# Moving background steps between the stages of the first section of a hybrid attention and retention trunk

## The chip, the cores and the metric

The kernel runs on one core of a Trainium2 chip. The metric is the device time of one execution, in microseconds (us). All times of the profile are of one execution on that core.

## The reference

The program is a trunk of two layers over a sequence of 2048 positions with 1024 features. Each layer normalises its input by its root mean square, projects it to eight groups of 512 columns, and feeds two mixers: chunked softmax attention (8 heads of 64 columns, each chunk of 64 positions seeing itself and the 8 chunks before it, with a relative bias) and multi-scale retention (4 heads of 128 columns, rotary phases, exponential decay from chunk to chunk). Both are gated, laid side by side, projected back and added to the input. Cut to what matters:

```python
hn = rms_norm(x, norm_gain)
proj = hn @ w_in                       # (2048, 1024) @ (1024, 4096)
aq, ak, av, ag, rq, rk, rv, rg = split(proj)
a = chunked_rel_attention(aq, ak, av, rel_bias) * silu(ag)
b = chunkwise_retention(rq, rk, rv, cos, sin) * silu(rg)
x = x + concat([a, b]) @ w_out         # and after two layers a last rms_norm
```

The rotary tables cos and sin are computed from the positions.

## The kernel before

All large products are made from 16-bit pieces: each operand is split in a high and a low part, and three products (high by high, high by low, low by high) are summed in PSUM.

A layer is done in four sections (s); a section is two attention heads and one retention head, 128 columns of each of the eight groups. Within a section the positions are done in four blocks (n) of 512. For each (layer, section, block) there are two stages on TensorE:

- the **T stage**, `dense_T` (L748): four products of 24 matmuls each, giving q, k, rq and rk with the columns on the partitions (tiles `dT`);
- the **V stage**, `dense_V` (L767): four products of 24 matmuls, giving v, rv and the gates with the positions on the partitions (tiles `dV`).

Each product is cut in three, so a stage has twelve "thirds" of 8 matmuls. After each third, `run()` does three things: it runs what had been put off to this third (`later`), it advances the attention generator of the block before by one step, and it pulls background steps. The attention generator brings the scores (matmuls L815 and L816; DVE L819 and L821; the exponential and a copy on ACT, L822 and L824; a subtraction on POOL, L825; a transposing DMA issued by SP, L827), the product with v (L835 to L837) and the retention (matmuls L869; copies on ACT L873; sums on DVE L877). A score unit has a name such as 2_1: the third run of 128 positions of the block, second head. Evacuations of the dense products are ACT and DVE instructions (L664, L667 and L681 in the T stage; L775 to L778 and L781 to L785 in the V stage). The rotary turn is three POOL instructions (L689 to L691).

The background steps are generators in a list, `bg`, and their order is the order in which they were pushed. At a third, `run()` pulls `ceil(todo / left)` steps, where `todo` is what remains of the pushed numbers of steps and `left` starts at the third argument of `run()` (the thirds over which the steps are to be spread) and falls by one with each third:

```python
            if bg:
                pull(min(-(-todo // max(left, 1)), todo))
            left -= 1
```

So a stage of twelve thirds that is run with 24 gets about half of what is outstanding, and one that is run with 12 gets all of it. A step issues its instructions at that point of the program, and each engine works through its instructions in program order. The order on each engine is thus set by these numbers.

In the first section of the first layer these are the background steps:

- `tables(n, ..)` (L85 to L128), for the rotary tables of a block: DVE steps, two sines on ACT (L117, L118; a load of the activation table stands before them and another when ACT goes back to its other functions), a negation (L120) and eight DMAs to memory (L125 to L128);
- `norms_from_input` (L1168 on), the input norms of four row tiles of 128 positions: load (L1177), a sum of squares on ACT (`sq`, L204), the mean on DVE (L209) and the power on POOL (L211), the multiplication on DVE (`mul`, L1189), the high part on ACT (`hi`, L226), the low part on DVE (`lo`, L230), and two transposing DMAs (L235, L236) into `hTh` and `hTl`, which the dense stages of that block read. At n = 1 they are for block 2 (row tiles 8 to 11), at n = 2 for block 3 (row tiles 12 to 15). In some of these steps the buffers of the high and low part are tiles named `rows`, in others tiles named `xa`;
- `prep_T` (25 steps), the weights of the next section for `dense_T`, in four parts: load (L297), a square with its sum on ACT (L312, its output goes to the tile `whT`), a cast on DVE (L319, `mbT`), a matmul with ones that adds over the partitions (L326, `msT`), a scale from it (L328, L143 to L147), and the two parts of the weights (L333 on ACT, `whT`; L336 on DVE, `wlT`);
- `prep_V` (23 steps), the same for `dense_V` (`msV` and so on), pushed at the last V stage of a section.

In the kernel before, `prep_T` of section 1 is pushed ahead of the T stage of block 3. T stages of this section are run with 10 (block 0), 22 (blocks 1 and 2) and 14 (block 3), V stages with 12, but with 24 for block 3.

Of the kernel before, what the change touches and what calls it, by code (L numbers as in the profile page):

```python
# [27 lines left out]
def hybrid_trunk(ctx: ExitStack, tc: tile.TileContext, x, pos, gain, gcol, w_in, w_out, rel, fgain,  # L28
# [6 lines left out]
    NS = SEQ // 512  # L35
    NSW = 4
# [348 lines left out]
    def prep_T(l, s, g, halves=False, w=None):  # L385
        w = w or Sections(l, s, g, halves)
        w.load(0)
        yield
        for j in range(4):
            if j < 3:  # L390
                w.load(j + 1)
            yield
            w.square(j)
            yield
            yield
            yield
            w.scale(j)
            yield from w.split(j)
# [208 lines left out]
    def later(k, fn):  # L607
        deferred.append([k, fn])
# [11 lines left out]
    def in_order(apart, terms):  # L620

        return [(kt, w) for w in terms for kt in range(KT)] if apart else [(kt, w) for kt in range(KT) for w in terms]
# [132 lines left out]
    def dense_V(l, s, n, g, st):  # L755
        hh, hl = hT[l, n]
        nm = f"{l}_{s}_{n}"
        st.v = b3.tile([P, 4, 2, 129], F16, tag="v", name=f"v{nm}")
        pool.memset(st.v[:, :, :, 64:65], 1.0)
        st.rv, st.g = [], []  # L760
        while g.vdone < 4:
            pull(1)
        for a in range(4):
            ps = psD.tile([P, 512], F32, tag="dense", name=f"dV{nm}_{a}")
            m = 0
            for kt, (w_, h_) in in_order(a == 0, ((g.vh, hh), (g.vh, hl), (g.vl, hh))):
                pe.matmul(ps, h_[:, kt, a * P:(a + 1) * P], w_[:, kt, :], start=(m == 0), stop=(m == 23))  # L767
                m += 1
                if m in (8, 16):
                    yield  # L770
            rv = gp.tile([P, 3, P], F16, tag="rv", name=f"rv{nm}_{a}")
            gt = gp.tile([P, 256], F32, tag="gt", name=f"gt{nm}_{a}")
            pv_ = ps[:, 0:P].rearrange("p (h d) -> p h d", h=2)
            vh_ = st.v[:, a, :, 0:64]
            act.activation(vh_, pv_, AF.Copy, scale=2.0 ** -16)  # L775
            act.activation(gt, ps[:, 256:512], AF.Tanh, scale=g.ugh[:, 0:1])
            act.activation(rv[:, 0], ps[:, P:256], AF.Copy, scale=g.urv[:, 0:1])
            act.activation(rv[:, 2], rv[:, 0], AF.Copy, scale=2.0 ** -11)  # L778

            def rests(a=a, ps=ps, pv_=pv_, vh_=vh_, rv=rv, gt=gt):  # L780
                dve.scalar_tensor_tensor(out=st.v[:, a, :, 65:129], in0=pv_, scalar=2.0 ** -16, in1=vh_,  # L781
                                         op0=ALU.mult, op1=ALU.subtract)
                dve.scalar_tensor_tensor(out=rv[:, 1], in0=ps[:, P:256], scalar=g.urv[:, 0:1], in1=rv[:, 0],
                                         op0=ALU.mult, op1=ALU.subtract)
                dve.scalar_tensor_tensor(out=gt, in0=gt, scalar=1.0, in1=ps[:, 256:512], op0=ALU.add, op1=ALU.mult)  # L785

            later(1, rests)
            st.rv.append(rv)
            st.g.append(gt)
            yield  # L790
# [342 lines left out]
    def push(gen, steps):  # L1133
        bg.append([gen, steps])

    def pull(k):
        for _ in range(k):
            while bg:
                try:
                    next(bg[0][0])  # L1140
                    bg[0][1] -= 1
                    break
                except StopIteration:
                    bg.pop(0)
# [7 lines left out]
    def grp(l, s):  # L1152
        if (l, s) not in groups:
            groups[l, s] = Grp()
        return groups[l, s]

    def run(gen, att, thirds):
        left = thirds
        for _ in gen:
            tick()  # L1160
            if att[0] is not None and next(att[0], att) is att:
                att[0] = None
            ring["att_done"] = att[0] is None
            todo = sum(max(b[1], 0) for b in bg)
            if todo == 0 and bg:
                todo = 1
# [3 lines that stand above are left out]
# [205 lines left out]
    att = [None]  # L1375
    for l in range(DEPTH):
        gO = [Grp(), Grp()]
        go = Grp()
        for s in range(NSW):
            g = grp(l, s)  # L1380
            for n in range(NS):
                first = (l, s, n) == (0, 0, 0)
                if not first:
                    st = St()
                    states[l, s, n] = st
                    dT = dense_T(l, s, n, g, st)
                else:
                    st = st0
                if n == 0 and not first:
                    bs, bt = bias_scratch(l, s), bias_tiles(l, s, g)  # L1390
                    later(1, lambda bs=bs: next(bs))
                    for k in (6, 10, 17, 21):
                        later(k, lambda bt=bt: next(bt))
                if (l, s) == (0, 0) and 0 < n < NS - 1:
                    if n == 1:
                        push(t1, TAB_STEPS - 7)
                    pairs = [xs0[0], w4.tile([P, D], F32, tag="w4", name="rows8") if n == 1 else xs0[1]]
                    pairs = [(w_[:, 0:D], w_[:, D:2 * D]) for w_ in (r_.bitcast(F16) for r_ in pairs)]
                    push(norms_from_input(range(4 * n + 4, 4 * n + 8), late[0:4] if n == 1 else None, pairs,
                                          tables(n + 1, [xs0[n + 1][:, i * 256:(i + 1) * 256] for i in range(4)])), 21)  # L1400
                if (l, s, n) == (0, 1, 1):
                    for l_ in range(1, DEPTH):
                        gr = gain_scale(l_)
                        later(2, lambda gr=gr: next(gr))
                        later(10, lambda gr=gr: next(gr))
                        later(18, lambda gr=gr: next(gr))
                if n == (NS - 1 if (l, s) == (0, 0) else 1):
                    if s + 1 < NSW:
                        push(prep_T(l, s + 1, grp(l, s + 1)), 25)
                    else:  # L1410
                        push(prep_O(l, 0, gO[0], go), 9)
                if n == NS - 1 and s == 1 and l + 1 < DEPTH:
                    gain_load(l + 1)
                if not first:
                    run(dT, att, 10 if n == 0 else 14 if (l, s, n) == (0, 0, NS - 1) else 22 if (l, s) == (0, 0) else 24)
                if n == NS - 1 and s == NSW - 1:
                    us = []
                    push(wout_first(l, go, us), 10)
                if n == 2 and s == 2:
                    push(prep_Omax(l, go), 13)  # L1420
                if n == NS - 1:
                    if s + 1 < NSW:
                        push(prep_V(l, s + 1, grp(l, s + 1)), 23)
                    else:
                        push(prep_O(l, 1, gO[1], go), 9)
                run(dense_V(l, s, n, g, st), att, 24 if n == NS - 1 and s < NSW - 1 else 12)
                if first:
                    sp_order.__exit__(None, None, None)
                    ring["free"] = True
                if att[0] is not None:  # L1430
                    drain(att[0])
                att = [attention(l, s, n, g, st, states.get((l, s, n - 1)))]
        pull(1000)
        if l + 1 == DEPTH:
            ring["fg"] = b3.tile([P, D], F32, tag="wh", name="fg")
            sp.dma_start(ring["fg"], fgain.to_broadcast([P, D]))
        wT = Sections(l + 1, 0, grp(l + 1, 0), True) if l + 1 < DEPTH else None
        wo = wout(l, go, gO, us, wT)

        def rounds_of(k):  # L1440
            run((next(wo) for _ in range(k)), att, k)

        rounds_of(30)
        if l + 1 < DEPTH:
            push(prep_T(l + 1, 0, grp(l + 1, 0), True, wT), 21)
            rounds_of(36)
            pull(1000)
            pV = prep_V_next(l + 1, grp(l + 1, 0))
            next(pV)
            rounds_of(18)  # L1450
            next(pV)
            rounds_of(6 * NT - 90)
            push(pV, 13)
        else:
            rounds_of(6 * NT - 36)
        run(wo, att, 15)
# [60 lines left out]
```

## Time and profile before

| | |
|---|---|
| time before, median of 3 runs | 2080.15 us (2079.01 to 2080.17) |
| profiled execution | 2082.83 us |
| its span in the trace | 2081.1 us |
| mean granted clock of TensorE | 0.991 of full speed |
| instructions | 39317 |

The stages around the change lie so in the trace of before, by the first matmul of each:

| stage | from, us | to, us |
|---|---|---|
| V stage of block 1 | 97.1 | 133.5 |
| T stage of block 2 | 133.5 | 160.4 |
| V stage of block 2 | 160.4 | 195.1 |
| T stage of block 3 | 195.1 | 225.2 |
| V stage of block 3 | 225.2 | 251.5 |

The engines are PE (TensorE; PEld is its weight load), DVE (VectorE), ACT (ScalarE), POOL (GpSimd) and SP (which issues the DMAs). In the page's slices each digit is the busy share of a fortieth of the span in tenths. In rows of the timeline the first number is the start and the second the duration in us; a bracket at the end gives the idle time of the engine ahead of the instruction and what ended it. A row of the table of windows gives the stretch, its length, and for each engine its busy time and the number of instructions, then TensorE's granted clock, the DMA engines' busy share and the GB/s. A row in the list of waits names the engine and its instruction, what it waited for, the total in us, the number of waits and the longest.

### The profile page before, as it was taken

Reading aid. Unit: us, or ns where it says so; the run is one execution under the profiler, and the core shown is the slowest. Engines: PE = TensorE matmul, PEld = TensorE weight load, DVE = VectorE, ACT = ScalarE, POOL = GpSimd, SP = SyncE. Lnnn points to the kernel's source line nnn. Section 1 sums busy time; section 2 is a strip of 40 time slices with the busy share of each in tenths; the row PEclk is TensorE's granted clock in tenths of the full one; section 3 lists DMA queues with packets and bytes.
Section 4 is the critical chain, followed back from the end, with each engine's and each line's share of the span. In section 5 each row is a group of like instructions: output and inputs, shape, how many; then the busy total and the mean of one; then the engine's idle time right before and its main releaser. Section 6 shows DMA issues by size and latency. Waiting matters only on the chain.

```text
span 2081.1 us, 39317 instructions
## 1 busy us (share of the span) xinstructions
PE 2006.5 (96%) x14014; PEld 1052.0 (51%) x14014; DVE 1229.8 (59%) x3817; ACT 1139.5 (55%) x2530; POOL 683.5 (33%) x701
## 2 busy tenths in 40 slices
PE   6988999999999999998999999999999999999998
PEld 4444545555555555544444555555555555554543
DVE  7776556566556555576653556555655565557643
ACT  7566665556565644555443546554655565446432
POOL 0244343444334434430002333444334334343100
PEclk9999999999999999999999999999999999999999
DMA  8678674547484854799765546554755776548874
GB/s 237 162 153 180 142 148 112 114 110 164 117 182 113 167 137 102 153 234 260 203 163 118 125 104 148 120 126 103 152 111 128 178 146 161 127 102 192 211 199 125
DMA packets 645701, 313.63 MB, mean 151 GB/s; under 512 B 459232, under 2 KB 602080, under 8 KB 645504
## 3 DMA queue, kind: packets, MB, share of 16 engines
q1 hardware_dynamic: 645504, 311.12, 65.5%
q8 instruction: 109, 1.79, 0.4%
q14 instruction: 88, 0.72, 0.1%
HBM read 123.26 MB, written 41.98 MB: 79 GB/s over the span
## 4 chain that ended last, share of the span: by engine, by line
PE 49%; DMA 2%; ACT 2%; DVE 1%; issue 0%; SPq 0%; POOL 0%; POOLq 0%; ACTq 0%; DVEq 0%
PE dT L748 15%; PE dV L767 14%; PE dO L1110 13%; PE r L869 2%; DMA pT<-pq 1%; PE S L816 1%; PE S L815 1%; PE o L835 1%; PE o L836 1%; PE o L837 1%; ACT stO1m L312 0%; ACT sc L822 0%; PE ptn L1011 0%; DVE sc L819 0%; ACT pq L824 0%
## 5 line engine op out<-in xcount | busy, mean ns | idle before, releaser
L825 POOL TENSOR_TENSOR pq<-sc,pq 128x640 f16<-128x640 f32 (+4 forms) x256 | 319.6, 1248 | 872.1 <-ACT pq L824 460.2
L822 ACT ACTIVATE sc<-sc,mq,cT 128x640 f32<-128x640 f32 (+4 forms) x256 | 218.4, 853 | 629.4 <-DVE rl L841 338.3
L767 PE MATMUL dV<-whV,hTh 128*128 128x512 f16 x1024 | 353.1, 381 | 4.3 <-DVE gt L785 4.2
L767 PE MATMUL dV<-wlV,hTh 128*128 128x512 f16 x1024 | 353.2, 381 | 0.0
L767 PE MATMUL dV<-whV,hTl 128*128 128x512 f16 x1024 | 353.1, 380 | 0.0
L748 PE MATMUL dT<-hTh,whT 128*128 128x512 f16 x1008 | 349.2, 382 | 2.1 <-DMA hTh<-xa 1.1
L748 PE MATMUL dT<-hTh,wlT 128*128 128x512 f16 x1008 | 348.0, 380 | 0.0
L748 PE MATMUL dT<-hTl,whT 128*128 128x512 f16 x1008 | 347.8, 380 | 0.0
L767 PEld LDWEIGHTS <-hTh 128*128 128x128 f16 x2048 | 196.8, 98 | 219.2 <-DVE gt L785 6.5
L748 PEld LDWEIGHTS <-whT 128*128 128x128 f16 x2016 | 193.0, 98 | 214.9 <-issue 10.6
L819 DVE CUSTOM_DVE_ANT_0 sc<-S,bias 128x640 f32<-128x640 f32 (+4 forms) x256 | 188.3, 736 | 112.7 <-PE S L816 111.3
L1110 PE MATMUL dO<-whO,yly 128*128 128x512 f16 x512 | 194.6, 380 | 1.5 <-DMA yly<-hTl 0.8
L1110 PE MATMUL dO<-whO,yhy 128*128 128x512 f16 x512 | 194.8, 381 | 1.0 <-DMA yhy<-hTh 1.0
L1110 PE MATMUL dO<-wlO,yhy 128*128 128x512 f16 x512 | 194.8, 380 | 0.0
L824 ACT ACTIVATE pq<-sc 128x640 f16<-128x640 f32 (+4 forms) x256 | 171.5, 670 | 8.1
L1110 PEld LDWEIGHTS <-yhy 128*128 128x128 f16 x1024 | 99.9, 98 | 116.1 <-DMA yhy<-hTh 1.5
L767 PEld LDWEIGHTS <-hTl 128*128 128x128 f16 x1024 | 99.3, 98 | 110.6 <-issue 1.9
L748 PEld LDWEIGHTS <-wlT 128*128 128x128 f16 x1008 | 97.5, 98 | 113.1 <-issue 6.2
L815 PE MATMUL S<-k,q 128*128 128x128 f16 (+3 forms) x592 | 142.9, 268 | 0.2
L835 PE MATMUL o<-v,pT 128*128 128x65 f16 x1120 | 130.0, 194 | 12.3 <-DMA pT<-pq 12.3
L836 PE MATMUL o<-v,pT 128*128 128x64 f16 x1120 | 130.2, 195 | 0.0
L816 PE MATMUL S<-k,q 128*128 128x128 f16 (+3 forms) x592 | 130.2, 268 | 0.0
(352 smaller groups left out, 3462.1 us busy)
## 6 DMA issues: line engine op xcount, KB each, us to landing
q<-qq SPq DMA_DIRECT2D x128, 128.0 KB, 2.4
yyy<-y_d SPq DMA_DIRECT2D x32, 512.0 KB, 4.7
stT<-in_w_in_dram SPq DMA_DIRECT2D x27, 512.0 KB, 5.1
stV<-in_w_in_dram SPq DMA_DIRECT2D x26, 512.0 KB, 4.7
k<-kk SPq DMA_DIRECT2D x128, 64.0 KB, 2.0
swp<-rot SPq DMA_DIRECT2D x64, 128.0 KB, 2.7
tabc<-tab SPq DMA_DIRECT2D x32, 256.0 KB, 3.0
tabs<-tab SPq DMA_DIRECT2D x32, 256.0 KB, 3.2
```

Of the source, the lines that this page charges most:

```text
L748: pe.matmul(ps, w_[:, j, kt, :], h_[:, kt, :], start=(m == 0), stop=(m == 23))
L767: pe.matmul(ps, h_[:, kt, a * P:(a + 1) * P], w_[:, kt, :], start=(m == 0), stop=(m == 23))
L815: pe.matmul(o, st.q[:, hx, 0, cs], k_, start=True, stop=False)
L816: pe.matmul(o, st.q[:, hx, 1, cs], k_, start=False, stop=True)
L819: dve.tensor_tensor_reduce(out=v, in0=S[:, 0:w], in1=g.bias[hx][:, 640 - w:640], scale=1.0, scalar=-3.0e38, op0=ALU.add, op1=ALU.max, accu ...
L822: act.activation(v, v, AF.Exp, bias=m[:, 0:1], scale=g.c[:, 0:1])
L824: act.activation(pq[:, 0:w], v, AF.Copy)
L825: pool.tensor_tensor(pq[:, w:2 * w], v, pq[:, 0:w], op=ALU.subtract)
L835: pe.matmul(o[:, 0:65], u.p[:, b, :], v_[:, 0:65], start=(b == 0), stop=False)
L836: pe.matmul(o[:, 0:64], u.p[:, b, :], v_[:, 65:129], start=False, stop=False)
L869: pe.matmul(out_, w_, m_, start=(i == 0), stop=(i + 1 == len(pairs)))
L1110: pe.matmul(ps, h_[:, kt, :], w_[:, kt, :], start=(m == 0), stop=(m == 23))
```

## The change

Three things change, all in layer 0, section 0. The T stages of blocks 1 and 2 are run with 16 instead of 22, so that more of the outstanding steps of norms and tables are pulled there and fewer are left to the V stages behind them. `prep_T` of section 1 is pushed after the T stage of block 2, that is, at the beginning of block 2's V stage, instead of before the T stage of block 3. And that V stage is run with 24 instead of 12, so that some half of the steps outstanding then is left to the T stage of block 3. For the other sections and the second layer the conditions give what they gave before.

```diff
-                if n == (NS - 1 if (l, s) == (0, 0) else 1):
+                if n == 1 and (l, s) != (0, 0):
                     if s + 1 < NSW:
                         push(prep_T(l, s + 1, grp(l, s + 1)), 25)
                     else:
...
                 if not first:
-                    run(dT, att, 10 if n == 0 else 14 if (l, s, n) == (0, 0, NS - 1) else 22 if (l, s) == (0, 0) else 24)
+                    run(dT, att, 10 if n == 0 else 14 if (l, s, n) == (0, 0, NS - 1) else 16 if (l, s) == (0, 0) else 24)
+                if (l, s, n) == (0, 0, NS - 2):
+                    push(prep_T(l, s + 1, grp(l, s + 1)), 25)
...
-                run(dense_V(l, s, n, g, st), att, 24 if n == NS - 1 and s < NSW - 1 else 12)
+                run(dense_V(l, s, n, g, st), att, 24 if (n == NS - 1 and s < NSW - 1) or (l, s, n) == (0, 0, NS - 2) else 12)
```

The numbers of instructions on each engine stay what they were. Of the matmuls only the six with ones (`msT`, and the first two `msV`) stand elsewhere in TensorE's order: the first `msT` stands in the V stage of block 2, in its second product, 8 matmuls behind the scores of unit 2_1 (of block 1's attention), the second at the end of the fourth product's second third there, the other two in the second and fourth product of block 3's T stage, each after 16 matmuls. On DVE, ACT, POOL and SP the steps change places with instructions of attention and of the evacuations between about 97 and 275 us of the trace of before.

## The prediction

> **What bounds the kernel now.** I write T2 for the T stage (dense_T) of block 2 and V2 for its V stage (dense_V), all in layer 0, section 0. First the page: its span, its busy times and its forty slices.
>
> ```profile
> span 2081.1 us, 39317 instructions
> PE 2006.5 (96%) x14014; PEld 1052.0 (51%) x14014; DVE 1229.8 (59%) x3817; ACT 1139.5 (55%) x2530; POOL 683.5 (33%) x701
> PE   6988999999999999998999999999999999999998
> ```
>
> PE is busy 96% of the span. The change moves work without adding any, so it can act only through PE's idle time and its clock, and the low digits stand in the slices up to some 200 us. Next the table of windows, one row for a stage: V1, T2, V2, T3, V3 (us, then busy time of PE, PEld, DVE, ACT, POOL, granted clock, DMA share).
>
> ```profile
> 97.10:133.50 36.40, 28.77 (x169) 13.72 (x168) 30.09 (x75) 22.96 (x53) 16.61 (x17) 0.91 0.70 157
> 133.50:160.40 26.90, 26.04 (x194) 13.73 (x195) 19.37 (x57) 14.91 (x32) 7.96 (x8) 1.00 0.84 156
> 160.40:195.10 34.70, 28.43 (x208) 15.21 (x205) 24.66 (x64) 22.08 (x47) 16.34 (x15) 0.95 0.80 186
> 195.10:225.20 30.10, 26.63 (x203) 14.13 (x204) 17.77 (x64) 20.08 (x41) 7.43 (x7) 1.00 0.78 174
> 225.20:251.50 26.30, 26.29 (x210) 14.50 (x208) 16.06 (x59) 15.66 (x39) 13.47 (x13) 1.00 0.49 115
> ```
>
> T2 and V3 are full of matmuls; V1, V2 and T3 hold PE idle for 7.6, 6.3 and 3.5 us. The list of PE's waits from 97 to 282 us says for what (us in total, times, longest).
>
> ```profile
> PE r L869 <- DVE sh L877: 5.7, 3, 4.2
> PE msT L326 <- DVE mbT L319: 3.4, 3, 1.7
> PE dV L767 <- DVE gt L785: 3.3, 1, 3.3
> ...
> PE dT L748 <- DMA hTh<-xa: 1.1, 1, 1.1
> PE o L835 <- DMA pT<-pq: 0.9, 1, 0.9
> ```
>
> So the helpers (DVE, ACT, POOL, SP) bound PE in these stages: they carry the background steps (norms and tables for later blocks, weights for section 1) in program order ahead of what PE needs next. Nothing that PE waits for is lost in the stages themselves; it is the order.
>
> **The change, part by part.** Instruction counts stay; the orders differ.
>
> *16 instead of 22 thirds.* In T1, 24 background steps are pulled instead of 22 (of 32); in T2, 17 instead of 12 (of 21). V2 keeps 4 of the norm steps instead of 9. What that puts on DVE and ACT in T2 I take from windows: V2, with its nine steps, held 24.66 us of DVE and 22.08 of ACT, V3, with none, 16.06 and 15.66. Five ninths of the differences are 4.8 us of DVE and 3.6 of ACT. T2 would then have 24.2 us of DVE and 18.5 of ACT in about 27, in order, with round trips from engine to engine. That is an estimate, and it says nearly full.
>
> *V1: a wait is made longer.* Rows of the timeline (start, duration):
>
> ```profile
> 107.25 1.32 POOL L691 TENSOR_TENSOR rot<-rot,swp 128x512 f32<-128x512 f32 x1
> 107.37 1.35 DVE L877 SCALAR_TENSOR_TENSOR sh<-sh,state 128x128 f16<-128x128 f16 x1
> 108.77 0.26 PE L869 MATMUL r<-sh,rot 128*128 128x128 f16 x1 [4.18 <-DVE sh L877]
> 108.83 0.27 DVE L877 SCALAR_TENSOR_TENSOR dT<-dT,r 128x128 f16<-128x128 f16 x1
> 110.09 0.66 POOL L211 TENSOR_TENSOR rsn<-ssn,mhalf 128x1 f32<-128x1 f32 x1
> ```
>
> By the changed order on DVE, the norm multiply (L1189) of row tile 10 now stands ahead of this L877, and it waits for its power on POOL (L211), which stands behind L691. L691 ends at 108.6; L211 0.66 makes 109.2; L1189 1.28 (its row is below) 110.5; a table step and L877, 0.27 each (the L877 of 108.83 has that length; the one of 107.37 ran beside L691), 111.0. PE's wait thus ends 2.3 us later. Behind the waiting L1189 stand only table steps and the retention's copies. Against it stand fewer steps at the end of V1 and the 0.9 us for pT, whose DMA goes out earlier; I take T2 as starting 1 us later. This does not go into the sum by itself, since the PE stops again later at a fixed point; it only moves that point.
>
> *The weights of section 1 from V2 on.* This is the deciding term. msT, the PE column sum (L326) of the first weight part, moves from the start of T3's second product to V2, 8 matmuls behind the scores of unit 2_1 (block 2 is under way, the unit belongs to block 1's attention). In PE's list this place is reached here:
>
> ```profile
> 169.46 0.22 PE L816 MATMUL S<-k,q 128*128 128x128 f16 x1
> ...
> 171.25 0.38 PE L767 MATMUL dV<-whV,hTl 128*128 128x512 f16 x1
> ```
>
> PE is in order, so whatever msT waits for, all matmuls behind it wait for. It needs ACT's square (L312) and DVE's cast (L319). In the changed order L312 stands behind ACT's exp and copy (L822, L824) of unit 2_1. And its output, whT, takes over the buffer of xa, so that it waits for the two transposes (L235, L236) of xa of row tile 15, the last of the norms. Where are they? Rows of before that price that chain:
>
> ```profile
> 166.58 0.21 DVE L821 TENSOR_SCALAR mq<-mq,ncT 128x1 f32<-128x1 f32 x1
> ...
> 174.57 0.82 DVE L819 CUSTOM_DVE_ANT_0 sc<-S,bias 128x640 f32<-128x640 f32 x1
> 175.56 1.22 DVE L230 TENSOR_TENSOR xa<-xin,xa 128x1024 f16<-128x1024 f32 x1
> ...
> 184.58 1.28 DVE L1189 SCALAR_TENSOR_TENSOR xin<-xin,rsn,gb 128x1024 f32<-128x1024 f32 x1
> ...
> 188.74 1.04 ACT L226 ACTIVATE xa<-xin 128x1024 f16<-128x1024 f32 x1
> 189.81 1.58 DVE L230 TENSOR_TENSOR xa<-xin,xa 128x1024 f16<-128x1024 f32 x1 [1.97 <-ACT xa L226]
> ...
> 193.13 1.29 SPq L236 DMA_TRANSPOSE hTl<-xa  x1
> ...
> 201.59 1.04 ACT L312 ACTIVATE whT<-stT 128x1024 f16<-128x1024 f32 x1
> ...
> 202.97 0.16 PE L326 MATMUL msT<-mbT,ones 128*128 128x1 bf16 x1 [1.32 <-DVE mbT L319]
> ```
>
> The landing time of that transpose is from the table of DMA issues (median us), the length of one issue of the tables' DMAs from the timeline.
>
> ```profile
> hTl<-xa SPq DMA_TRANSPOSE x3, 3.1
> ```
>
> ```profile
> 181.51 0.59 SPq L126 DMA_DIRECT2D tab<-xb  x1
> ```
>
> In the changed order tile 15's multiply (before at 184.58) stands right behind the L821 of 166.58, so it has moved by seventeen places of attention work. Without any lag it would start near 166.8. I add the 1 us from V1 and a lag of 5 us: before, in V2, the same steps had made DVE's L819 start at 174.57, 4.9 us behind the end of its scores (169.46 + 0.22). So 172.8. Then L1189 1.28, L226 1.04, L230 1.22 and some 0.6 between them: 177.0. From the end of L230 to the second landing it took 193.13 + 3.1 - (189.81 + 1.58) = 4.8 us: 181.8. On SP the transposes are moved past the tables' eight issues, two swaps and the transpose of pT (2_0); these are queued just ahead, and I charge three issues, 1.7 us: 183.5. L312 to msT took 202.97 - 201.59 = 1.4: msT is released at **R = 184.9**, against 171.2 where PE has its place in before. PE arrives 1 us late from V1, and later by what T2's fuller queues make it wait (3 us, a guess; it comes off msT's wait and leaves R alone): near 175, to wait some 10 us. The weight loads (L297), which go out earlier, are needed only after that; they lie hidden, and if their cover were gone they would move R no further than x15's landing does.
>
> *V2 with 24 thirds, T3 and V3 with one step per third.* What PE waited for later in V2 is late no more, because DVE and ACT clear their queues while PE stands at msT:
>
> ```profile
> 174.71 0.23 PE L869 MATMUL r<-rv,dT 128*128 128x128 f16 x1 [1.29 <-DVE dT L877]
> 184.72 0.39 PE L767 MATMUL dV<-whV,hTh 128*128 128x512 f16 x1 [3.26 <-DVE gt L785]
> 193.68 0.23 PE L869 MATMUL r<-rv,dT 128*128 128x128 f16 x1 [0.69 <-DVE dT L877]
> 255.29 0.16 PE L326 MATMUL msV<-mbV,ones 128*128 128x1 bf16 x1 [0.70 <-DVE ya L847]
> ```
>
> Gone: 1.29 + 3.26 + 0.69 in V2, the 1.1 for hTh at T3's start (its transposes land ten us earlier), the 3.4 of msT in T3 (halved step rate; parts 0 and 1 are already done), and 0.70 of msV, one step earlier. That is 10.4 us. Bounds: each could stay whole (nothing gone where DVE is as late as before), and I take them as gone because V3 in before, with one step per third, held PE busy for 26.29 of 26.30 us.
>
> *The clock.* After a long wait PE runs at half clock, as two stretches show:
>
> ```profile
> 110.00:114.00 4.00, 4.00 (x17) 1.59 (x16) 3.79 (x11) 0.53 (x3) 0.66 (x2) 0.50 0.92 229
> 114.00:116.00 2.00, 2.00 (x11) 0.95 (x10) 1.50 (x7) 0.72 (x2) 0.00 (x0) 0.97 1.25 265
> 186.00:188.00 2.00, 2.00 (x20) 1.22 (x18) 1.73 (x8) 0.86 (x1) 0.00 (x0) 0.50 0.62 168
> 188.00:190.00 2.00, 2.00 (x13) 1.10 (x11) 0.19 (x1) 1.97 (x4) 1.09 (x1) 0.70 0.43 156
> ```
>
> The 4.18 us wait cost 4 x 0.50 + 2 x 0.03 = 2.1 us more; the 3.26 us one cost 2 x 0.5 + 2 x 0.3 = 1.6. I charge 2.1 behind msT and give back 1.6. A rule on this: the Trainium skill, "TensorE: Matmul & The Clock Gate", Part 1, says that the clock falls to half only after an idle window of about 3.4 us. By it the 3.26 us wait would have no tail to give back, and the sum would come out 1.6 us higher; the row at 186 us shows 0.50 behind that wait, so here the trace decides against it.
>
> **The sum.** R moves PE by 184.9 - 171.2 = 13.7; the clock adds 2.1; gone are 10.4 + 1.6 = 12.0: **+3.8 us**. The profiled execution took 2082.83 us (span 2081.1 and 1.7 around it), which would make 2086.6; against the median of 2080.15, 2.7 lower, it is **2084**. About 0.2% (4.2 us) is what a measurement of this kernel can tell from no change, and the forecast lies just inside it.
>
> Bounds: with R as early as 174 (no lag, the chain of exp and copy alone) msT hardly waits, there is no tail, and 2.8 - 12.0 = -9; with R at 189 it is 17.8 + 2.1 - 12.0 = +8, and with some of the 3.4 of msT left in T3, +10.
>
> **Rivals.** *Faster: the helpers keep up.* T3 in before has its L819 on the heels of the scores. If T2 takes the five steps without lag, tile 15's multiply starts near 167.8; 4.1 + 4.8 us later, 176.7, the landing; R = 178.1 or earlier, and 6.9 + 2.1 - 12.0 = -3, without the tail -5: about 2076. For it: T2 has a third of DVE's time free in before. Against it: V2 in before lags with the same steps. It decides at the L819 of unit 2_1: if it starts within 2 us of its scores, this is the case.
>
> *Slower, clearly: SP or POOL holds tile 15 longer.* Each norm multiply waits for a power that stands on POOL among the subtractions of pq, whose group on the page is this:
>
> ```profile
> L825 POOL TENSOR_TENSOR pq<-sc,pq 128x640 f16<-128x640 f32 (+4 forms) x256 | 319.6, 1248 | 872.1 <-ACT pq L824 460.2
> ```
>
> If the round trips of tiles 13, 14 and 15 in T2 each cost one such subtraction more, R comes 3 x 1.25 = 3.7 later, 188.6, and the sum is +7.5: 2087.7. It is this case if tile 15's second transpose lands past 186.
>
> *Little comes of it: the waits change places.* Two of 32 and five of 21 steps move; if SP's queue is clear when tile 15 arrives, R is 182 or 181 and the sum is between 0 and +1: 2080 to 2081.
>
> **Chances.** Forecast (R 183 to 187, +2 to +6) 0.42; little 0.20; faster 0.18; clearly slower 0.20. The range 2075 to 2090 takes in the rivals and leaves out the floor and the end beyond +10. Of the forecast's own chance over half lies past +4.2, with the slower rival 0.44; the faster rival lies partly within the bound, but the floor adds to it: 0.18; 0.38 remains for within 0.2%.
>
> **What the next profile would show.** In the list of PE's waits, msT <- mbT of 8 to 10 us in V2 and none over 0.5 in T3; gt L785 gone; sh L877 6.4 instead of 4.2 in V1; the granted clock at 0.5 for some 4 us behind msT; T3 about 26.7 us long and V2 about 40. A msT wait under 4 us, msT waits left in T3, or a new wait of PE inside T2 that isn't swallowed by msT's would make it wrong.

## The result, and the profile after

Five runs of the changed kernel took 2085.85 to 2093.35 us, median 2089.43; five of the kernel before, timed beside them, 2078.61 to 2083.89, median 2080.15. The ratio is 1.0044, with a 95% interval of 1.0026 to 1.0061: slower by some 0.4%. The profiled execution took 2085.85 us, the shortest of the five, with a span of 2084.0 us. A later repetition with eleven runs (below) gave 1.0025 [1.0015, 1.0036]. The two intervals share 1.0026 to 1.0036, that is 5.4 to 7.5 us.

The table of windows of the changed kernel, by its own stages: V1, T2, V2, T3, V3, and then the T and V stage of block 0 of section 1 (stretch, length, busy time of PE, PEld, DVE, ACT, POOL, granted clock, DMA share, GB/s).

```profile
97.40:135.60 38.20, 28.55 (x169) 13.80 (x168) 30.92 (x79) 24.78 (x57) 17.59 (x18) 0.87 0.76 171
135.60:165.90 30.30, 27.74 (x198) 14.66 (x196) 22.70 (x61) 14.52 (x31) 7.95 (x9) 0.94 0.69 138
165.90:206.40 40.50, 27.93 (x209) 14.53 (x206) 21.16 (x69) 25.54 (x51) 14.79 (x14) 0.87 0.78 171
206.40:232.60 26.20, 26.20 (x207) 14.15 (x205) 15.47 (x56) 15.28 (x34) 6.70 (x6) 1.00 0.69 150
232.60:259.00 26.40, 26.29 (x209) 14.33 (x207) 19.19 (x57) 17.54 (x42) 14.19 (x13) 1.00 0.61 132
259.00:285.70 26.70, 26.32 (x206) 14.01 (x204) 16.29 (x56) 18.51 (x44) 6.99 (x8) 1.00 0.86 181
285.70:312.10 26.40, 26.04 (x204) 14.10 (x201) 16.54 (x54) 16.49 (x40) 15.05 (x16) 1.00 0.74 147
```

The same two stages of section 1 in before, of which the prediction counted one wait (0.70 us for msV):

```profile
251.50:280.50 29.00, 26.65 (x206) 14.17 (x204) 15.80 (x61) 19.87 (x46) 6.98 (x8) 1.00 0.77 185
280.50:310.30 29.80, 27.77 (x205) 14.70 (x202) 17.26 (x54) 16.97 (x40) 15.03 (x16) 0.94 0.70 122
```

T3 now is full of matmuls (26.20 busy of 26.20). V2 holds PE idle for 12.6 us instead of 6.3, T2 for 2.6 instead of 0.9, and the two stages of section 1 lost nearly all of theirs. PE's waits from 97 to 290 us in the changed kernel:

```profile
PE msT L326 <- DVE mbT L319: 11.9, 1, 11.9
PE r L869 <- DVE sh L877: 6.7, 2, 5.6
PE r L869 <- ACT dT L873: 2.6, 1, 2.6
PE dT L748 <- DVE kk L667: 2.6, 1, 2.6
PE o L835 <- DMA pT<-pq: 0.8, 2, 0.4
```

All of the wait for gt, the three waits for msT in T3 and those for dT in V2 are gone. (kk is the k that the T stage evacuates, gt the gates, sh the retention's state as an operand of its matmuls, pT the transposed exponentials of the scores.) One wait for msT of 11.9 us stands in their place. Its chain, from the timeline of the changed kernel, in order of time:

```profile
170.19 1.31 POOL L689 TENSOR_TENSOR rot<-rot,tabc 128x512 f32<-128x512 f32 x1 [0.91 <-DMA y_d<-yr]
...
172.81 1.27 POOL L691 TENSOR_TENSOR rot<-rot,swp 128x512 f32<-128x512 f32 x1
...
174.03 0.55 POOL L211 TENSOR_TENSOR rsn<-ssn,mhalf 128x1 f32<-128x1 f32 x1
...
174.62 1.28 DVE L1189 SCALAR_TENSOR_TENSOR xin<-xin,rsn,gb 128x1024 f32<-128x1024 f32 x1 [2.88 <-POOL rsn L211]
...
177.79 1.22 DVE L230 TENSOR_TENSOR xa<-xin,xa 128x1024 f16<-128x1024 f32 x1
...
182.25 1.36 SPq L827 DMA_TRANSPOSE pT<-pq  x1
183.71 1.25 SPq L235 DMA_TRANSPOSE hTh<-xa  x1
185.05 1.29 SPq L236 DMA_TRANSPOSE hTl<-xa  x1
...
188.34 1.06 ACT L312 ACTIVATE whT<-stT 128x1024 f16<-128x1024 f32 x1 [4.39 <-DMA hTl<-xa]
...
189.52 0.16 DVE L319 CAST mbT<-m1T 128x1 bf16<-128x1 f32 x1 [7.29 <-ACT whT L312]
189.73 0.16 PE L326 MATMUL msT<-mbT,ones 128*128 128x1 bf16 x1 [11.90 <-DVE mbT L319]
```

Read it from below: PE waits for the cast, that for ACT's square, that for the landing of the last transpose of xa, whose buffer it overwrites; the transpose stood on SP for 6 us after its data were complete (179.0 to 185.05); and row tile 15's multiply had waited 2.88 us for a power that stood behind POOL's rotary turn.

### The profile page after: what moved, and what is told of

It reads as the page before. It is cut to its first block, busy times and chain, and to the rows that moved or that the text cites. A ratio compares the mean times of both kernels' runs of the same rounds, so it can differ in the third digit from the quotient of the medians.

```text
span 2084.0 us, 39309 instructions
## 1 busy us (share of the span) xinstructions
PE 2002.5 (96%) x14014; PEld 1051.0 (50%) x14014; DVE 1234.1 (59%) x3817; ACT 1139.0 (55%) x2530; POOL 683.1 (33%) x701
## 4 chain that ended last, share of the span: by engine, by line
PE 48%; DMA 2%; ACT 2%; DVE 1%; issue 1%; POOL 0%; SPq 0%; POOLq 0%; ACTq 0%; DVEq 0%
PE dT L748 15%; PE dV L767 13%; PE dO L1110 13%; PE r L869 2%; DMA pT<-pq 1%; PE S L815 1%; PE S L816 1%; PE o L835 1%; PE o L836 1%; PE o L837 1%; ACT sc L822 0%; ACT stO1m L312 0%; DVE sc L819 0%; PE ptn L1011 0%; POOL pq L825 0%
## 5 line engine op out<-in xcount | busy, mean ns | idle before, releaser
L822 ACT ACTIVATE sc<-sc,mq,cT 128x640 f32<-128x640 f32 (+4 forms) x256 | 218.5, 853 | 625.4 <-DVE rl L841 336.2
L819 DVE CUSTOM_DVE_ANT_0 sc<-S,bias 128x640 f32<-128x640 f32 (+4 forms) x256 | 188.5, 736 | 106.9 <-PE S L816 105.2
L824 ACT ACTIVATE pq<-sc 128x640 f16<-128x640 f32 (+4 forms) x256 | 171.5, 670 | 8.1
L815 PE MATMUL S<-k,q 128*128 128x128 f16 (+3 forms) x592 | 142.9, 268 | 0.2
L835 PEld LDWEIGHTS <-pT 128*128 128x128 f16 x1120 | 105.6, 97 | 53.2 <-DMA pT<-pq 25.0
```

The lines of the kernel that those rows point to most:

```text
L815: pe.matmul(o, st.q[:, hx, 0, cs], k_, start=True, stop=False)
L819: dve.tensor_tensor_reduce(out=v, in0=S[:, 0:w], in1=g.bias[hx][:, 640 - w:640], scale=1.0, scalar=-3.0e38, op0=ALU.add, op1=ALU.max, accu ...
L822: act.activation(v, v, AF.Exp, bias=m[:, 0:1], scale=g.c[:, 0:1])
L824: act.activation(pq[:, 0:w], v, AF.Copy)
L835: pe.matmul(o[:, 0:65], u.p[:, b, :], v_[:, 0:65], start=(b == 0), stop=False)
```

## The experiments

All were timed in several rounds beside the kernel before on the same chip; the ratio is to that kernel. Stage lengths are from the first matmul of a stage to the first of the next, read from the timelines. The first two columns are two executions of the kernel before, the third and fourth two of the changed one. The medians were not all taken beside the same runs of before; the kernels are compared by their ratios.

| stage, us | before | again | after | rep | t16 | n2only | early | sqwl | late | late22 | late18 | n1at22 |
|---|---|---|---|---|---|---|---|---|---|---|---|---|
| V1 | 36.4 | 35.8 | 38.2 | 38.2 | 37.6 | 36.1 | 36.4 | 39.1 | 39.5 | 34.0 | 36.1 | 36.4 |
| T2 | 26.9 | 26.6 | 30.3 | 30.2 | 30.3 | 30.3 | 26.1 | 30.3 | 30.3 | 30.3 | 27.5 | 30.3 |
| V2 | 34.7 | 34.6 | 40.6 | 40.3 | 35.7 | 36.1 | 44.2 | 36.3 | 38.5 | 37.8 | 40.5 | 41.6 |
| T3 | 30.1 | 30.2 | 26.1 | 26.1 | 29.8 | 29.8 | 26.1 | 26.6 | 26.1 | 26.1 | 26.1 | 26.1 |
| V3 | 26.3 | 26.3 | 26.4 | 26.4 | 26.3 | 26.3 | 27.6 | 30.1 | 26.9 | 26.7 | 26.3 | 26.4 |
| T, block 0, section 1 | 29.0 | 29.0 | 26.7 | 26.6 | 29.0 | 29.0 | 27.0 | 26.1 | 27.3 | 27.5 | 29.0 | 27.1 |
| V, block 0, section 1 | 29.8 | 29.9 | 26.5 | 27.1 | 27.9 | 26.9 | 27.1 | 26.6 | 26.8 | 27.3 | 27.2 | 27.1 |
| median time | 2080.15 | 2082.83 | 2089.43 | 2085.85 | 2086.44 | 2086.27 | 2083.52 | 2084.18 | 2083.43 | 2079.99 | 2082.53 | 2083.70 |

**The changed kernel again (rep).** No edit.

> The changed kernel once more, as a control for the others and for the scatter: its five runs went from 2085.85 to 2093.35 us, and the one with the profile was the fastest. The theory that msT's wait of 11.9 us (for the buffer that xa leaves) and what follows it decides expects 2086 to 2090 us again, a wait of msT on mbT of 11 to 12.5 us at the same place, and L312 released by the landing of hTl from xa. The rival that half-clock stretches falling by chance made the difference of the medians expects a median below 2085 us here.

2085.85 us (2082.76 to 2093.39, 11 runs) against 2081.03; ratio 1.0025 [1.0015, 1.0036]. The median lies just between the two forecasts (2086 or more, below 2085). The waits of msT, sh and kk came back to within 0.2 us; msT in V2:

```profile
PE msT L326 <- DVE mbT L319: 11.8, 1, 11.8
```

So these waits come back with the program's order, and the change is slower in repetition, if by less than the first five runs said.

**Only the T stages with 16 (t16).**

```diff
-  ... 14 if (l, s, n) == (0, 0, NS - 1) else 22 if (l, s) == (0, 0) else 24)
+  ... 14 if (l, s, n) == (0, 0, NS - 1) else 16 if (l, s) == (0, 0) else 24)
```

> Only the T stages of blocks 1 and 2 with 16 instead of 22; prep_T of section 1 is pushed where it was before, and block 2's V stage runs with 12. The theory that msT decides expects 2079 to 2083 us: the later end of the T stage of block 2 (5 us in the trace of after: 2 from the sh wait, 3 from the kk wait) stays, but the gt wait of 3.3 us with its half clock goes and nothing new comes. The rival that the denser T stages are the harm, and the weights' place innocent, expects 2085 us or more, with the T stage of block 2 ending 5 us late and nothing of that given back.

2086.44 us, ratio 1.0030 [1.0018, 1.0042]. This went to the rival: half the change, without the early weights, costs as much as all of it. The wait for gt did go, but the V stage of block 2 became no shorter (35.7 us), because waits for pT took its place. PE's waits in t16 from 130 to 200 us:

```profile
PE o L835 <- DMA pT<-pq: 5.5, 3, 2.9
PE dT L748 <- DVE kk L667: 2.6, 1, 2.6
PE r L869 <- DVE dT L877: 1.5, 1, 1.5
```

**Only the early weights (early).** The T stages keep 22; the rest is as changed.

> Only the other half: prep_T of section 1 pushed at block 2's V stage, which runs with 24, and T stages with 22 as before. Nine steps of the norms are then still ahead of prep_T, pulled two per third, and msT stands 24 matmuls later in the order than in after. The theory that msT waits for xa's last transposes expects a wait of msT on mbT of 7 to 14 us in that V stage and 2084 to 2089 us in all, although the T stage of block 2 ends as in before (160 us). The rival that the denser T stages are the harm expects 2078 to 2082 us and a msT wait below 4 us.

2083.52 us, ratio 1.0013 [1.0001, 1.0024], between the two forecasts. T2 ends as in before and V2 is the longest of all, 44.2 us. PE's waits in that run from 155 to 206 us:

```profile
PE r L869 <- ACT dT L873: 6.2, 1, 6.2
PE msT L326 <- DVE mbT L319: 5.2, 2, 4.8
PE r L869 <- DVE dT L877: 2.3, 1, 2.3
```

msT waits 4.8 us at the first place, also between the two, because PE is held 6.2 us earlier by L873, which stands on ACT behind a norm step and two loads of activation tables. (The expectation of the run "late" says that this L873 stood behind L312; its timeline shows L873 at 178.7 and L312 at 192.5, so that was misread.) The stage loses 9.5 us and the four stages behind it give 4.0 back in T3, 2.0 and 2.7 in section 1, and lose 1.3 in V3.

**The square's unused output elsewhere (sqwl).**

```diff
-  self.sq[j] = lowp(sumsq(self.sts[j], nm, self.g.h[:, j]), nm)
+  self.sq[j] = lowp(sumsq(self.sts[j], nm, (self.g.l if (self.l, self.s) == (0, 1) else self.g.h)[:, j]), nm)
```

> The changed kernel, but the squares of section 1's weights (L312) write their unused output into the tile wlT instead of whT, so that the square does not wait for xa's buffer (wlT takes over the tables' buffer, whose last DMA was issued at 180.3 us in after). All else is in the same order. The theory that the buffer holds msT expects the wait of msT to fall from 11.9 to about 7.5 us (then ACT's copy L824, which ended at 183.95 us, is what it waits for, plus 1.4 us) and the time to fall by 4 us against the repeated run of the changed kernel. The rival that ACT's and DVE's lag holds it expects 11 us or more still and no change. If the conversion L333, which still needs the buffer, merely takes the wait over, a new wait of PE on ACT or DVE of 2 to 4 us appears later in that stage.

PE's wait and three ACT instructions in this run:

```profile
PE msT L326 <- DVE mbT L319: 7.2, 1, 7.2
```

```profile
182.63 0.92 ACT L822 ACTIVATE sc<-sc,mq,cT 128x640 f32<-128x640 f32 x1 [2.95 <-DVE mq L821]
...
184.22 1.04 ACT L312 ACTIVATE wlT<-stT 128x1024 f16<-128x1024 f32 x1
...
189.97 1.15 ACT L333 ACTIVATE whT<-stT,sT 128x1024 f16<-128x1024 f32 x1 [3.90 <-DMA hTl<-xa]
```

The wait fell by 4.6 us as the buffer theory said, V2 by 4.0 (36.3 against 40.3), and L333 took over the wait for the buffer without holding PE. This shows that the buffer held the end of msT's wait. In the other 7.2 us L312 stood right behind L822 and L824 on ACT, and L822 had itself waited 2.95 us for DVE. The time moved less: 2084.18 us, 1.0020 [1.0011, 1.0029] against 1.0025 of the repetition, the intervals overlapping. In the profiled execution a wait for pT of 2.1 us with half clock behind it stood in V3 (30.1 us; no other run in the table has more than 27.6).

**The tables' last steps held back (tabend).**

```diff
-            next(tab, None)
+            if not (ts[0] == 12 and 15 <= r <= 17):
+                next(tab, None)
```

> The changed kernel with three steps of the last tables held back, so that their eight DMAs are issued behind the transposes of row tile 15 instead of ahead of them. The theory that msT waits for the landing of these transposes, and that SP's queue is what makes them late, expects the second transpose to go out near 180 to 182 us instead of 185.05, and the wait of msT to fall from 11.8 us to 7 to 9 us, where ACT's copy L824 holds it; V stage of block 2 3 to 4 us shorter than 40.3 us, time 3 us under the repeated changed kernel. The rival that the transposes are late because xa's low part (L230) or the DMA engines are late expects 11 us still.

2085.85 us, 1.0011 [0.9999, 1.0023]. PE waited 11.1 us for msT, V2 took 40.0 us, and the transpose went out at 184.46, in a V2 that began 1.9 us later than in after. This looked like the rival, but the experiment was not clean: the steps held back hold the sines too, so that ACT came to L824 only at 189.18 and to L312 at 189.82, with no wait for a DMA any more. The edit thus put a new holder in the place of the one that it took away, and does not show what SP's queue alone costs.

**The weights seven thirds later (late), with 22 for block 1 (late22, late22b), with 18 for block 2 (late18).**

```diff
-                    push(prep_T(l, s + 1, grp(l, s + 1)), 25)
+                    later(7, lambda s=s: push(prep_T(0, s + 1, grp(0, s + 1)), 25))
```

In late22 and late22b the number is `(22 if n == 1 else 16)`, in late18 `(22 if n == 1 else 18)` with `later(8, ..)`.

> The changed kernel, but prep_T of section 1 is pushed seven thirds later in block 2's V stage; msT then stands 32 matmuls, 7 us, later in PE's order. The theory that PE only waits because it comes too early expects msT's wait to fall from 11.8 to 2 to 5 us, the V stage of block 2 to be 33 to 36 us long instead of 40.3, the T stage of block 3 to stay at 26 to 27 us, and 2079 to 2082 us in all. The rival that another wait takes its place (as in the run with the weights alone early, where PE waited 6.2 us for ACT's L873, behind L312) expects a V stage of 38 us or more. The denser T stages' 5 us (sh and kk) stay in either case.

> As the run before it, but the T stage of block 1 runs with 22 as in the kernel before (block 2's with 16). The theory that the 24 steps in that stage put the norm multiply of tile 10 ahead of L877 expects the V stage of block 1 to take 36.4 us again instead of 38.2, with the sh wait at 4.1 instead of 5.6, and the kk wait of 2.6 us in the T stage of block 2 to stay; time 2 us under the run before it. The rival that the V stage's length comes from the end of the tables expects 38 us.

late: 2083.43 us, 1.0002 [0.9989, 1.0016]; late22: 2079.99, 0.9989 [0.9979, 1.0000]. In late, msT waits 1.8 us, but V2 is 38.5 us, at the bound named for the rival: pT took its place. PE's waits in late22, from 155 to 200 us:

```profile
PE o L835 <- DMA pT<-pq: 5.8, 4, 3.1
PE r L869 <- DVE dT L877: 2.4, 2, 1.5
PE msT L326 <- DVE mbT L319: 0.8, 2, 0.5
```

The V stage of block 1 shrank by more than the 2 us expected (34.0 against 39.5). Its waits account for it: for dT from ACT and twice for sh, 2.8 + 4.7 + 2.5 us in late, for sh alone 3.6 + 0.7 + 0.8 in late22. But up to the end of this stage DVE and ACT have the same order in late22 as in before, n2only, early, late18 and n1at22, where it takes 35.8 to 36.4 us. So the number 22 brings V1 back to about 36, and the 2 us below that are not shown to be the edit's.

> The run with 22 for block 1, 16 for block 2 and the weights pushed seven thirds later, once more, since it was the only one under the kernel before (ratio 0.9989, interval up to 1.0). If that holds, 1 to 4 us under before again, with the V stage of block 2 at 38 us and the T stage of block 3 at 26.1; if it was chance, equal or above. Its V stage of block 1, 34.0 us then, should be nearer to 36, as in the two traces of before.

2080.34 us, 1.0005 [0.9992, 1.0017], V1 again 34.2: the gain did not repeat, the stage length did. This version is level with the kernel before. Against the changed one in repetition (1.0025 [1.0015, 1.0036]) late22 is faster; the interval of late22b just touches it.

> As the run with 22 for block 1 and the weights pushed late, but block 2's T stage with 18 instead of 16, and the push one third later (8 instead of 7). In its order L667 stands ahead of the norm multiply of row tile 13, not behind it. The theory that L667 waits behind that multiply, which waits for its power, expects the kk wait of 2.9 us to be gone, the T stage of block 2 at 27 us instead of 30.3, and the time 1 to 3 us under that of the run with 16; with fewer steps taken early, the T stage of block 3 may take 1 to 3 us more than 26.1. The rival that the engines are simply too full in that stage expects another wait there and 30 us still.

2082.53 us, 1.0012 [1.0000, 1.0025]. The kk wait is gone and T2 takes 27.5 us, as expected; nothing is won, for V2 takes 40.5, with these waits from 130 to 200 us:

```profile
PE o L835 <- DMA pT<-pq: 6.3, 2, 3.2
PE r L869 <- DVE dT L877: 2.9, 3, 1.6
PE msT L326 <- DVE mbT L319: 2.3, 1, 2.3
```

**Only block 2's stage with 16 (n2only).**

> The kernel before with one number changed: 16 instead of 22 for the T stage of block 2 alone (block 1's stays at 22, prep_T where it was). It parts the dearer half of the denser T stages. The theory that block 2's kk wait costs most expects the T stage of block 2 at 30.2 us (26.8 before), the V stage of block 1 at 36 us, the stages from 71 to 310 us 2 to 3 us longer than before's 237 to 239, and a time 2 to 4 us above before. The rival that block 1's stage makes the 6 us of the run with both at 16 expects no more than 1 us above before.

2086.27 us, 1.0028 [1.0015, 1.0040], T2 30.3 us, V1 36.1. As much as with both stages at 16: block 2's stage alone is enough for the harm in time, and block 1's adds little. The stages from 71 to 310 us took 239.2 us against 237.1 and 238.9 of before, 1 us longer where 2 to 3 were expected, while the time rose by 5.9 us, above the 2 to 4 expected: what the trace of one execution shows and what the times show differ here too.

**Block 1 back at 22 in the changed kernel (n1at22).**

> The changed kernel with the T stage of block 1 back at 22 and all else as changed: it takes out the sh wait alone and gives the later stages another profile. The theory that the stages add up expects the V stage of block 1 at 36 us instead of 38.2, the T stage of block 2 at 30.3, its V stage at 39 to 41 with msT waiting 11 to 12 us, block 3's T stage at 26.1, and the time 2 to 3 us under the repeated changed kernel's distance from before (4.8 us), so 2 to 3 us above before. The rival that the later waits only absorb what the sh wait delayed (msT's release being set by POOL, SP and ACT, not by PE's arrival) expects the V stage of block 2 to become 2 us longer and no gain in all.

2083.70 us, 1.0018 [1.0007, 1.0028], against 1.0025 of rep: no clear difference. V1 fell by 1.8 us as expected, and V2 rose by 1.2 us. V1, T2 and V2 together took 108.3 us against 109.0 in after and 108.8 in rep, so most of it was given back, as the rival had it. Its mechanism fell all the same: msT waited 11.9 us as before although PE came to it 1.5 us earlier, counted from V1's first matmul, so its release moved along. A part of the 1.2 us is the clock behind msT. It was 0.50 from 189.5 to 194 us and 0.97 from 194 to 196, which cost 2.3 us, against 1.5 in after and 1.9 in rep. The rest is not settled, and the two ratios' intervals overlap, so the expected gain of 2 us is neither shown nor excluded.

**The kernel before against itself (again).**

> The kernel before against itself, for the scatter and for a second profile. Expected: the ratio's interval holds 1, width about 0.2%. In the first profile the V stage of block 0 of section 1 took 29.8 us with a wait of 2.0 us for pT and half clock behind it, where the four other traces show 26.5 to 27.9: if that was chance, it takes 26.5 to 28 us here, and the stages from 71 to 310 us (238.9 us in the first profile) take about 236. All the other stages within 0.5 us of the first profile.

1.0005 [0.9992, 1.0017]; 2079.95 to 2089.25 us. The V stage of block 0 of section 1 took 29.9 us again with the pT wait, so this was hardly chance: every execution of another kernel took 26.5 to 27.9 us there. The other stages of the table agree within 0.7 us.

## Why the prediction was right, and where it was off

The forecast was 2084 us, 3.8 us slower, with msT's wait for xa's buffer as the deciding term. The direction held, and msT's wait came by the mechanism named: L312 was released by the landing of hTl from xa, and sqwl, which only takes that buffer away, shortened the wait by 4.6 us. By size the first measurement (9.3 us by the medians) is over twice the forecast, the repetition (4.8) close to it. That closeness is partly luck, for two errors work against each other: msT's release came 4.8 us later than forecast, and the stages of section 1 gave back more than was counted.

That msT's wait decides the time is not shown. Runs without that wait in V2 (t16, n2only) are as slow as the change, and sqwl, which shortens it by 4.6 us, is not clearly faster. late, with 1.8 us of it left, came out lower (1.0002 [0.9989, 1.0016] against 1.0025 [1.0015, 1.0036]), though in V2 pT took a part of its place. The waits are explained by the runs, the time only in part.

By its steps, stage lengths against the mean of the two executions of before, and the changed ones as the mean of after and rep:

- **V1, the sh wait.** L1189 stood where the changed order put it. The rows of after:

```profile
107.74 1.32 POOL L691 TENSOR_TENSOR rot<-rot,swp 128x512 f32<-128x512 f32 x1
109.03 0.54 POOL L211 TENSOR_TENSOR rsn<-ssn,mhalf 128x1 f32<-128x1 f32 x1
109.60 1.29 DVE L1189 SCALAR_TENSOR_TENSOR hTl<-hTl,rsn,gb 128x1024 f32<-128x1024 f32 x1 [0.94 <-POOL rsn L211]
110.80 1.00 DVE L113 TENSOR_SCALAR xb<-xb 128x256 f32<-128x256 f32 x1
...
111.73 0.28 DVE L877 SCALAR_TENSOR_TENSOR sh<-sh,state 128x128 f16<-128x128 f16 x1
112.06 0.27 PE L869 MATMUL r<-sh,rot 128*128 128x128 f16 x1 [5.57 <-DVE sh L877]
```

  The chain is the predicted one; L113 took 1.00 instead of 0.27, and L877 ended at 112.0 instead of 111.0. Of the 6.4 us forecast for one wait, 5.6 show at sh and 1.3 more in a wait of 2.6 just ahead (1.3 before). The stage grew by 38.2 - 36.1 = 2.1 us.
- **T2.** The 3 us for its fuller queues, called a guess, were a wait of 2.6 for kk with 30.3 x 0.06 = 1.8 us of half clock behind it (the granted clock of the stage was 0.94 instead of 1.00), and the mechanism is the same as in V1: L667 behind a multiply that waits for its power.

```profile
154.56 0.66 POOL L211 TENSOR_TENSOR rsn<-ssn,mhalf 128x1 f32<-128x1 f32 x1 [2.46 <-DVE ssn L209]
155.25 1.28 DVE L1189 SCALAR_TENSOR_TENSOR xin<-xin,rsn,gb 128x1024 f32<-128x1024 f32 x1 [0.44 <-POOL rsn L211]
...
156.79 0.68 DVE L667 SCALAR_TENSOR_TENSOR kk<-dT,kk 128x512 f16<-128x512 f32 x1
```

  The stage grew by 30.2 - 26.8 = 3.5 us, the 0.9 us for pT being gone. late18, where L667 stands ahead of that multiply, has no such wait. The prediction had named a new wait in T2 as a sign against it, unless msT's wait swallows it, and had said that it "leaves R alone". No run tests that by itself. In two pairs the stages T2 and V2 together took nearly the same with the wait and without it: 70.8 and 70.5 us in after and rep against 70.3 in early, 68.1 in late22 against 68.0 in late18, though other steps moved in these pairs too. n1at22 shows only that R is no fixed point: V1 ended earlier there, and R came earlier by the whole 1.5 us.
- **R, the mis-sized term.** Forecast 184.9, measured 189.7. The working had tile 15's multiply at 172.8. In after DVE was done with the L821 ahead of it at 171.74, so the 5 us of lag and the 1 us from V1 were enough, but the multiply started at 174.62, as its power stood behind POOL's turn (170.19 to 174.08), which the working left out. From the end of L230 (179.0) to L312 (188.34) it took 9.3 us, against 4.8 + 1.7 in the sum: SP issued the tables' DMAs, two swaps and pT first. Together that is 1.8 + 2.8 of the 4.8 us. So the slower rival's outcome (R = 188.6) came, and its sign too (a landing past 186, which was at about 188.3), by POOL's turn and SP's queue and not by its three subtractions of pq. The faster rival's sign failed: L819 of unit 2_1 started 5 us behind the end of its scores (175.88 + 0.22), as late as in before.

```profile
181.15 0.82 DVE L819 CUSTOM_DVE_ANT_0 sc<-S,bias 128x640 f32<-128x640 f32 x1
```

- **What goes.** The 3.4 us of msT in T3, the 1.1 of hTh, the waits of V2 and the 0.7 of msV went as forecast: T3 fell from 30.1 to 26.1.
- **The clock.** Half clock stood behind the waits, and it also set in during msT's wait, where it costs nothing:

```profile
178.00:182.00 4.00, 0.00 (x0) 0.00 (x0) 3.98 (x11) 1.25 (x5) 0.55 (x1) 1.00 0.42 100
182.00:186.00 4.00, 0.00 (x0) 0.00 (x0) 0.21 (x1) 1.66 (x2) 1.97 (x2) 0.54 0.95 202
...
189.70:192.00 2.30, 2.27 (x7) 0.89 (x7) 1.09 (x8) 1.65 (x3) 0.00 (x0) 0.50 1.17 326
192.00:194.00 2.00, 2.00 (x16) 1.04 (x14) 0.01 (x1) 0.91 (x4) 0.00 (x0) 0.85 1.87 212
```

  Behind msT it cost 2.3 x 0.50 + 2 x 0.15 = 1.5 us, 2.1 having been charged.
- **What the prediction left out.** The first two stages of section 1 gained 2.3 and 3.0 us. In the first, before had two waits for msV:

```profile
PE msV L326 <- DVE ya L847: 2.2, 2, 1.5
```

  The prediction counted the one of 0.7 us and passed over the other. Where the weights are ready late (t16, n2only, late18) both waits stay, of 0.7 and 1.5 us, and the stage takes 29.0, so that gain is the early weights'. In the second stage a wait of 2.0 us for pT, with half clock behind it, shrank to 0.4 (1.0 in rep). The prediction took that stage as unchanged. Its gain appears in every variant, with early weights or without; what makes pT ready sooner is not settled.

The sum of the stages: +2.1 +3.5 +5.8 -4.0 +0.1 -2.3 -3.0, unrounded +2.0 us, where +3.8 was forecast. The first five came to +7.4, and the last two gave 5.4 back, of which 0.7 had been counted. Against the medians, +4.8 and +9.3, at least 1 us is missing: rep's lower bound is 0.0015 x 2081 = 3.1 us. The profiles are single executions and don't show where it is. Behind these stages the kernel before took 1770.8 us in one execution and 1776.8 in the other, the changed one 1771.9 and 1770.6. Half clock is not what these traces show as the cause: in windows of 5 us behind 310 us, up to the last matmul, it lies at 875, 970, 1490 and 1630 us in before, and only at 890, 975 and 1635 in after. Where the rest of the time lies stays open.

Where the expected gain went, then: the change takes some 10 us of waits out of V2 and T3, but the helpers have the same work. In run after run a wait went at one place and another came: gt to pT (t16), gt and the msT of T3 to kk and the msT of V2 (after), msT to pT (late), kk to pT (late18).

## What to carry to other kernels

A background step that waits on another engine (here a multiply waiting for POOL's power) holds everything queued behind it on its own engine; look in the new order for such a step just ahead of an instruction that PE needs. When a step is moved early, look up who last used its output buffer: an output that nobody reads, as that of this square, still waits for it. And when PE's waits come from full helpers, taking one wait away shows the next; measure the whole stretch, with the stages behind it, and repeat both kernels, before a change of 0.2% is believed.

## What the runs showed of the hardware

The same wait of 3.26 us for gt stood in both executions of the kernel before. In the first, the granted clock was 0.50 behind it (quoted in the prediction); in the second it stayed at 1.00. The second execution of before, PE's wait and the clock behind it:

```profile
185.06 0.39 PE L767 MATMUL dV<-whV,hTh 128*128 128x512 f16 x1 [3.26 <-DVE gt L785]
```

```profile
186.00:188.00 2.00, 2.00 (x27) 1.30 (x26) 1.89 (x9) 0.52 (x1) 0.00 (x0) 1.00 0.48 107
188.00:190.00 2.00, 2.00 (x11) 0.92 (x10) 0.17 (x1) 1.97 (x3) 0.76 (x1) 1.00 0.67 223
```

So the prediction was too quick to let one row decide: a wait of about this length may or may not cost the 1.6 us. The Trainium skill, "TensorE: Matmul & The Clock Gate", Part 1, calls the window in which TensorE's activity is watched free-running, not tied to the kernel's start. With that these two executions agree, while the first one's 0.50 behind a wait shorter than the page's idle window of 3.4 us does not. The times scatter too: one and the same kernel before went from 2075.17 to 2088.32 us in 35 runs.
